# A late output transfer and one more side step between the S5 and dt stages of a hybrid SSD, S5 and attention kernel

## The chip, the cores and the metric

The kernel runs on 1 core of one Trainium2 chip. Its time is the device time of one execution in microseconds (us); the time before is the median of 3 runs.

## What is computed

One layer of a streaming encoder works on 528 prompt rows and 64 sample rows of 1024 channels. After a norm, one wide projection feeds three branches: a Mamba-2 scan (SSD) with heads weighted by `dt`, an S5 state-space branch with a GLU, and stick-breaking attention. The lifted branches are gated and summed, projected back, and followed by an MLP:

```python
y_a, conv_new, ssd_new = ssd_branch(h, ...)
y_b, s5_re, s5_im = s5_branch(h @ col(OFF_U, S5_WIDTH), ...)
glu = jax.nn.gelu(y_b) @ lp['w_glu']
out_b = glu[..., :D_MODEL] * jax.nn.sigmoid(glu[..., D_MODEL:])
o_c = stick_breaking(q, k, v)
mix = (gates[:, :, 0] * (y_a @ lp['w_lift_a']) + gates[:, :, 1] * out_b
       + gates[:, :, 2] * (o_c @ lp['w_lift_c']))
x = x + mix @ lp['w_out']
x = x + jnp.square(jax.nn.relu(rmsnorm(x) @ lp['w_up'])) @ lp['w_down']
```

The states of the branches are outputs too; the final S5 states go out as `s5_out`.

## The kernel before

TensorE works through a list of dense projections (`dense`, L379): each weight tile of 128x1024 is loaded (`w_raw`, L287), split by ScalarE into a high part (`w_hi`, L253) and by VectorE into a low part (`w_lo`, L217), and multiplied in three passes per 128 rows of contraction (L336 to L338), 24 matmuls for a part of 288 columns (12 for the GLU and the attention lift, whose contraction is half as long). Three PSUM buffers (`ps_d`) hold the sums until they are evicted. The order of the projections is: u, q/v/k, then xbc, z and the gates g1, g2, g0, then `glu`, `lc` (the attention lift, input `ocx`), `la` (the SSD lift, inputs `yah` and `yal`), `out`, and the MLP.

The scans and the attention are side work. They are Python generators that yield between steps: `s5_parts`, `s5`, `attention` (which first runs `steps`, the dt sums) and `ssd`. After each dense part, `side` (L373) adds the front generator's pace to a credit and lets it do one step (`pull`) for each whole unit; the paces are 1.25, 1.35, 1.8 and 1.1 (L35). The steps are traced in this order, and a scheduler of the framework then places every instruction into its engine's queue by its own estimate of readiness. What stands in a queue afterwards is therefore not fixed by the source line alone.

The places that the change touches: `s5` computes its end states into `so` (L814 to L816), sends them to `s5_out` (L817), and then runs eight steps `it` that load a tile `tz` from DRAM (L834) and do the last S5 matmuls `ps_y` (L847, L849). `attention` (L885) calls `steps` (L1139): the matmuls of dt (`ps_dt`, L1148), two exponentials on VectorE (`expd`, tiles `ea_` and `ed_`), a softplus (`sp_`), `dta` (L1182) and the dt sums on TensorE (`ps_ac`, L1184 to L1186). Then come four attention tiles, and after them `ssd`: six chunks with `turned`, `decay`, `weigh`, `outputs` (`ps_y`, L1318) and `state`, and between them `gated` and `normed`, which multiply with z, sum squares into `sa`, take a norm by a matmul with ones (`ps_n`, L408) and an rsqrt on ScalarE and VectorE (`rstd_of`, L240 to L247), and scale `ya`. At the end `yah` and `yal` (L257, L258) are split off for `la`:

```python
for g in range(2):
    normed(1, g)
    yield
    for m in range(4 * g, 4 * g + 4):
        scaled_split(ya[:, m, on], sg[:, m:m + 1], yah[:, m, on], yal[:, m, on])
```

The norm matmul occurs four times in `ssd`; the fourth is the last of the side work on TensorE before `la`.

Of the kernel before, what the change touches and what calls it, by code (L numbers as in the profile page):

```python
# [176 lines left out]
def body(tc, io):  # L177
    nc = tc.nc
    V, S, G, PE, SP = nc.vector, nc.scalar, nc.gpsimd, nc.tensor, nc.sync
# [4 lines left out]
    with ExitStack() as ctx:  # L184
# [31 lines left out]
        def tt(e, o, a, b, op):  # L216
            e.tensor_tensor(o, a, b, op=op)  # L217
# [31 lines left out]
        def sigmoid(a, out, scale=1.0):  # L249
            S.activation(out, a, AF.Sigmoid, scale=scale)  # L250
# [469 lines left out]
        def s5():  # L720
# [93 lines left out]
            so = new("so", [128, 4, 16])  # L814
            for j, (xx, c) in enumerate(((x_r, NB), (x_i, NB), (x_r, NX - 1), (x_i, NX - 1))):
                G.tensor_copy(so[:, j, :], xx[:, :, c])  # L816
            SP.dma_start(io["s5_out"], so)  # L817
            yield

            y_sb = sp.tile([128, 32, NY], F32, name="y_sb", tag="yy")  # L820
# [8 lines left out]
            for it in range(8):  # L829
                t0, gl = 4 * (it // 2), it % 2  # L830
                gs = slice(2 * t0 + gl, 2 * t0 + 8, 2)
                tz = sp.tile([128, 4, 128], F32, name="tz", tag="tz%d" % (it % 2))
                for s in range(8):
                    SP.dma_start(tz[16 * s:16 * s + 16, :, :], kv[:, gs, (7 - s) * 16:(7 - s) * 16 + 128])  # L834
                oc = sp.tile([128, 4, 8, 16], F32, name="oc", tag="oc%d" % (it % 2))
                od = sp.tile([128, 4, 8, 16], F32, name="od", tag="od")
                sh = [128, 4, 8, 16]
                for e, o, j in ((V, oc, 0), (G, od, 1)):
                    tt(e, o, p2[j][:, gl, :, t0:t0 + 4].rearrange("p s t -> p t s").unsqueeze(3).to_broadcast(sh),
                       cc[:, j].rearrange("p (h t c) -> p h t c", h=2, c=16)[:, gl, t0:t0 + 4].unsqueeze(2)  # L840
                       .to_broadcast(sh), OP.mult)
                tt(V, oc, oc, od, OP.add)
                yield
                ps = psg.tile([128, 512], F32, name="ps_y5", tag="g")
                for j in range(4):
                    o = ps[:, j * NY:(j + 1) * NY]
                    PE.matmul(o, tz[:, j, :], ub[:, 2 * (t0 + j) + gl, MB + 1:NX], start=True, stop=False,  # L847
                              skip_group_check=True)
                    PE.matmul(o, fs(oc[:, j]), xs[gl][:, t0 + j, MB:NX - 1], start=False, stop=True, skip_group_check=True)  # L849
                yield  # L850
                pv = ps[:, :4 * NY].rearrange("p (g b) -> p g b", b=NY)
                yv = y_sb[:, gs, :]
                c0 = 2.0 * math.sqrt(2.0 / math.pi)
                sq = sp.tile([128, 4 * NY], F32, name="gsq", tag="gsq")
                S.activation(sq, ps[:, :4 * NY], AF.Square)
                V.scalar_tensor_tensor(sq, sq, 1.0 / 0.044715, ps[:, :4 * NY], op0=OP.add, op1=OP.mult)
                sigmoid(sq, sq, 0.044715 * c0)
                tt(V, yv, pv, sq.rearrange("p (g b) -> p g b", b=NY), OP.mult)
                if it % 2:
                    m = it // 2  # L860
                    yo = yb_scr[128 * m:128 * m + 128, :].rearrange("(g c) (s b) -> s c g b", c=16, b=NY)
                    for s in range(8):
                        SP.dma_start(yo[s], y_sb[16 * s:16 * s + 16, 8 * m:8 * m + 8, :])
                yield
# [18 lines left out]


        def attention():  # L885
            yield from steps()
            ap = tc.alloc_tile_pool(name="attn", bufs=2)
            a1 = tc.alloc_tile_pool(name="attn1", bufs=1)
# [534 lines left out]
        n1.release()  # L1423
        do_dt()
        pulls.append((s5(), PACE["s5"]))
        for m in range(4):
            do_qk("q", m, qg, q_scr, live)
            do_v(m)
            do_qk("k", m, kg, io["k_out"], halves)
        pulls.append((attention(), PACE["attention"]))  # L1430
        for n, m in mixed():
            if n == "xbc":
# [229 lines left out]
```

## Time and profile before

| | us |
|---|---|
| median of 3 runs | 1118.86 (1118.25 to 1122.1) |
| profiled execution, device time | 1120.97 |
| its span, first to last instruction | 1119.2 |
| TensorE busy in the span | 1100.5 |
| VectorE busy | 794.3 |
| ScalarE busy | 539.6 |

The span is what the rows below divide up; 1.8 us of the profiled execution lie around it. The profiled execution is 2.1 us above the median of the runs. A busy matmul row lasts about 0.3 us, but they overlap and follow each other at about 0.13 us.

### The profile page before, as it was taken

The numbers are of one execution on the slowest core, as the hardware profiler recorded it, in microseconds if no ns is written. First come the engines' busy times: TensorE is split into PE (matmuls) and PEld (weight loads), VectorE is DVE, ScalarE is ACT, GpSimd is POOL, SyncE is SP. The second block draws the span as 40 slices with busy tenths as digits, with TensorE's granted clock in tenths as the row PEclk, the third lists the DMA queues.
The fourth block names the chain that finished last, engine by engine and source line by source line (L and its number), as shares of the span: only waits on it lengthen the run. The fifth ranks groups of instructions, "written<-read, shape, count | busy, mean of one in ns | idle before, by whom it ended". The sixth has DMA issues, their size and how long they took to land.

```text
span 1119.2 us, 21309 instructions
## 1 busy us (share of the span) xinstructions
PE 1100.5 (98%) x8532; PEld 1061.7 (95%) x8532; DVE 794.3 (71%) x1377; ACT 539.6 (48%) x896; POOL 183.7 (16%) x240
## 2 busy tenths in 40 slices
PE   9999999999999999999998999999999999999998
PEld 8998999999998999898788999999999999999998
DVE  7968579955667475549988754467866785786787
ACT  6455465523365455465668323355444444444443
POOL 2086256611000000005422300300000000000000
PEclk9999999989999999999999999999999999999999
DMA  7663224466754353277445543322232223223222
GB/s 275 147 145 115 84 90 125 110 165 165 241 177 138 113 179 133 89 255 257 129 146 167 151 134 99 99 75 94 76 102 88 75 77 115 74 76 129 79 81 80
DMA packets 80594, 144.04 MB, mean 129 GB/s; under 512 B 26512, under 2 KB 40688, under 8 KB 79984
## 3 DMA queue, kind: packets, MB, share of 16 engines
q1 hardware_dynamic: 80496, 142.69, 41.0%
q8 instruction: 67, 1.10, 0.4%
q14 instruction: 31, 0.25, 0.1%
HBM read 117.40 MB, written 24.38 MB: 127 GB/s over the span
## 4 chain that ended last, share of the span: by engine, by line
PE 80%; DVE 10%; POOL 3%; ACT 2%; DMA 2%; issue 2%; SPq 1%; DVEq 0%; ACTq 0%; POOLq 0%
PE ps_d L336 18%; PE ps_d L337 18%; PE ps_d L338 18%; PE ps_x L1581 3%; PE ps_x L1580 3%; PE ps_x L1582 3%; PE ps_o L895 2%; PE ps_z L895 2%; PE ps_y L1581 1%; PE ps_y L1580 1%; PE ps_y L1582 1%; DVE w_lo L217 1%; DVE ar L1272 1%; DVE ar L217 1%; POOL cm L217 1%
## 5 line engine op out<-in xcount | busy, mean ns | idle before, releaser
L336 PE MATMUL ps_d<-hh,w_hi 128*128 128x288 f32 (+1 forms) x864 | 260.5, 301 | 0.0
L338 PE MATMUL ps_d<-hh,w_lo 128*128 128x288 f32 (+1 forms) x864 | 260.0, 301 | 0.0
L337 PE MATMUL ps_d<-hl,w_hi 128*128 128x288 f32 (+1 forms) x864 | 260.0, 301 | 0.0
L253 ACT ACTIVATE w_hi<-w_raw 128x1024 fp32r<-128x1024 f32 (+1 forms) x150 | 151.8, 1012 | 220.7 <-PE ps_d L337 142.8
L217 DVE TENSOR_TENSOR w_lo<-w_raw,w_hi 128x1024 fp32r<-128x1024 f32 (+1 forms) x150 | 179.2, 1195 | 104.2 <-ACT w_hi L253 103.7
L337 PEld LDWEIGHTS ps_d<-hl,w_hi 128*128 128x128 f32 x864 | 164.5, 190 | 0.9 <-issue 0.3
L338 PEld LDWEIGHTS ps_d<-hh,w_lo 128*128 128x128 f32 x864 | 164.7, 191 | 0.5
L336 PEld LDWEIGHTS ps_d<-hh,w_hi 128*128 128x128 f32 x864 | 164.7, 191 | 0.4
L336 PE MATMUL ps_d<-x2h,w_hi 128*128 128x288 f32 x512 | 151.3, 296 | 0.0
L337 PE MATMUL ps_d<-x2l,w_hi 128*128 128x288 f32 x512 | 151.1, 295 | 0.0
L338 PE MATMUL ps_d<-x2h,w_lo 128*128 128x288 f32 x512 | 150.3, 295 | 0.0
L338 PEld LDWEIGHTS ps_d<-x2h,w_lo 128*128 128x128 f32 x512 | 96.2, 188 | 0.1
L336 PEld LDWEIGHTS ps_d<-x2h,w_hi 128*128 128x128 f32 x512 | 96.2, 188 | 0.1
L337 PEld LDWEIGHTS ps_d<-x2l,w_hi 128*128 128x128 f32 x512 | 96.2, 188 | 0.0
L253 ACT ACTIVATE w_hi<-ws 128x1024 fp32r<-128x1024 f32 x32 | 34.0, 1061 | 55.0 <-PE ps_y L1581 21.7
L1581 PE MATMUL ps_x<-ftl,w_hi 128*128 128x288 f32 x192 | 56.7, 295 | 0.5 <-DVE ftl L217 0.5
L1580 PE MATMUL ps_x<-fth,w_hi 128*128 128x288 f32 x192 | 56.8, 296 | 0.2 <-ACT s L1600 0.2
L1582 PE MATMUL ps_x<-fth,w_lo 128*128 128x288 f32 x192 | 56.4, 294 | 0.0
L1531 ACT ACTIVATE fr<-ps_d 128x288 f32<-128x288 f32 x64 | 25.7, 402 | 55.8 <-PE ps_d L338 55.8
L217 POOL TENSOR_TENSOR xe<-xd,tend 128x1024 f32<-128x1024 f32 (+2 forms) x6 | 11.6, 1942 | 234.4 <-DVE xd L217 210.1
L217 DVE TENSOR_TENSOR w_lo<-ws,w_hi 128x1024 fp32r<-128x1024 f32 x32 | 39.0, 1220 | 12.6 <-ACT w_hi L253 12.6
L906 DVE TENSOR_TENSOR_SCAN aw<-col,aw 128x400 f32<-128x400 f32 (+4 forms) x36 | 30.7, 899 | 17.3 <-ACT aw L250 17.2
(472 smaller groups left out, 2727.1 us busy)
## 6 DMA issues: line engine op xcount, KB each, us to landing
w_raw<-wts SPq DMA_DIRECT2D x150, 512.0 KB, 3.5
g_scr<-go SPq DMA_DIRECT2D x24, 288.0 KB, 2.8
gt<-g_scr SPq DMA_DIRECT2D x24, 288.0 KB, 3.1
ar<-ac_scr SPq DMA_DIRECT2D x4, 1024.0 KB, 7.2
x_scr<-cs SPq DMA_DIRECT2D x10, 297.5 KB, 2.9
xc<-x_scr SPq DMA_DIRECT2D x4, 640.0 KB, 7.0
xt<-xT SPq DMA_DIRECT2D x8, 296.0 KB, 5.7
z_scr<-zs SPq DMA_DIRECT2D x8, 288.0 KB, 4.6
```

Source lines behind the costliest of these rows:

```text
L217: e.tensor_tensor(o, a, b, op=op)
L253: S.activation(hi, x, AF.Copy)
L336: PE.matmul(ps, wh[:, c], xh[:, k, cols], start=start and k == 0, stop=False)
L337: PE.matmul(ps, wh[:, c], xl[:, k, cols], start=False, stop=False)
L338: PE.matmul(ps, wl[:, c], xh[:, k, cols], start=False, stop=stop and k == kt - 1)
L895: mm = lambda *a, **b: PE.matmul(*a, skip_group_check=True, **b)
L906: V.tensor_tensor_scan(x, one.to_broadcast([128, n]), x, 1.0, op0=OP.mult, op1=OP.mult)
L1272: V.tensor_scalar(ar[:n, h, :n], ar[:n, h, :n], acm[:n, c, h:h + 1], 0.0, op0=OP.subtract, op1=OP.min)
L1531: S.activation(r[:, cols], ps, AF.Relu)
L1580: PE.matmul(ps, w[0][:, o], fh[:, k], start=first and k == 0, stop=False, skip_group_check=True)
L1581: PE.matmul(ps, w[0][:, o], fl[:, k], start=False, stop=False, skip_group_check=True)
L1582: PE.matmul(ps, w[1][:, o], fh[:, k], start=False, stop=k == 3, skip_group_check=True)
```

## The change

The call that sends the S5 end states is moved from before the eight S5 steps into the one with `it == 4`, and the attention generator gets one empty step before the dt sums.

```diff
@@ in s5
             for j, (xx, c) in enumerate(((x_r, NB), (x_i, NB), (x_r, NX - 1), (x_i, NX - 1))):
                 G.tensor_copy(so[:, j, :], xx[:, :, c])
-            SP.dma_start(io["s5_out"], so)
             yield
...
                 od = sp.tile([128, 4, 8, 16], F32, name="od", tag="od")
+                if it == 4:
+                    SP.dma_start(io["s5_out"], so)
                 sh = [128, 4, 8, 16]
@@ in attention
         def attention():
+            yield
             yield from steps()
```

In the queues this is what comes of it. On SyncE, where the DMAs are issued, the rows around `s5_out` (its name is `s_out` here, its source `so`), first before:

```order
L287 DMA w_raw<-wts 128x1024
L828 DMA xs_2385<-x_r 64x1216
L828 DMA xs_2384<-x_i 64x1216
L817 DMA s_out<-so 128x64
L287 DMA w_raw<-wts 128x1024
L578 DMA x_scr<-cs 128x595
```

and now, with the line numbers of the changed file:

```order
L287 DMA w_raw<-wts 128x1024
L827 DMA xs_2384<-x_r 64x1216
L827 DMA xs_2383<-x_i 64x1216
L837 DMA s_out<-so 128x64
L287 DMA w_raw<-wts 128x1024
L578 DMA x_scr<-cs 128x595
```

The transfer has kept its place in the queue, the 99th of SyncE's DMAs and branches in both. TensorE's queue also is the same row for row up to and including the dt matmuls `ps_dt`.

On VectorE, between the end of the second exponential (`e_`) and the softplus (`sp_`), before:

```order
L276 SCALAR_TENSOR_TENSOR e_3367<-ed_q,ed_b 128x96
L217 TENSOR_TENSOR w_lo<-w_raw,w_hi 128x1024
L1165 TENSOR_SCALAR s_3368<-e_3367 128x96
L217 TENSOR_TENSOR akcl<-akc,akch 128x512
L1166 RECIPROCAL s_3368<-s_3368 128x96
L217 TENSOR_TENSOR akcl<-aks,akch 128x64
L217 TENSOR_TENSOR qbl<-aqs,qbh 64x64 x2
L217 TENSOR_TENSOR s_3368<-s_3368,e_3367 128x96
L217 TENSOR_TENSOR s_3369<-s_3368 128x96
L1169 TENSOR_SCALAR sp__3394<-s_3369 128x96
L1171 SCALAR_TENSOR_TENSOR sp__3394<-sp__3394,s_3369 128x96 x6
L217 TENSOR_TENSOR w_lo<-w_raw,w_hi 128x1024
```

and now:

```order
L276 SCALAR_TENSOR_TENSOR e_3402<-ed_q,ed_b 128x96
L1167 TENSOR_SCALAR s_3403<-e_3402 128x96
L1168 RECIPROCAL s_3403<-s_3403 128x96
L217 TENSOR_TENSOR s_3403<-s_3403,e_3402 128x96
L217 TENSOR_TENSOR s_3404<-s_3403 128x96
L1171 TENSOR_SCALAR sp__3429<-s_3404 128x96
L1173 SCALAR_TENSOR_TENSOR sp__3429<-sp__3429,s_3404 128x96 x6
L217 TENSOR_TENSOR w_lo<-w_raw,w_hi 128x1024
```

The splits of the first attention tile's sample keys (`akcl`, `qbl`) have left this stretch for a later one, and the chain reaches `dta` one weight split earlier. The two exponentials, which stood one after the other, are now interleaved. On TensorE the dt sums `ps_ac`, and with them the first attention tile, come 48 dense matmuls earlier than before; the four tiles then drift between 60 earlier and 80 later, and the last attention matmul and the first of `ssd` stand 2 earlier than before. From there the SSD outputs `ps_y` stand 17 to 25 dense matmuls later, those of the last chunk 57; the four norm matmuls `ps_n` stand 38, 27, 82 and 55 later, so that 77 dense matmuls lie between the fourth and `la`, where 132 lay before. ScalarE's queue has 37 table loads where it had 35.

On VectorE, at the end of the side work, from the fourth norm (`rsl`) to the last `yal` (`gt<-ps_d` are evictions of `lc`), before:

```order
L246 SCALAR_TENSOR_TENSOR rsl<-ps_n,rsl 128x288
L217 TENSOR_TENSOR gt<-ps_d,gt 128x288
L217 TENSOR_TENSOR w_lo<-w_raw,w_hi 128x1024
L247 SCALAR_TENSOR_TENSOR sa<-rsl,sa 128x288
L217 TENSOR_TENSOR gt<-ps_d,gt 128x288 x2
L217 TENSOR_TENSOR ya<-ya,sa 128x288 x4
L217 TENSOR_TENSOR gt<-ps_d,gt 128x288
L258 SCALAR_TENSOR_TENSOR yal<-ya,sg,yah 128x576 x2
L217 TENSOR_TENSOR gt<-ps_d,gt 128x288
L258 SCALAR_TENSOR_TENSOR yal<-ya,sg,yah 128x576 x2
```

and now:

```order
L246 SCALAR_TENSOR_TENSOR rsl<-ps_n,rsl 128x288
L217 TENSOR_TENSOR w_lo<-w_raw,w_hi 128x1024
L217 TENSOR_TENSOR gt<-ps_d,gt 128x288
L247 SCALAR_TENSOR_TENSOR sa<-rsl,sa 128x288
L217 TENSOR_TENSOR gt<-ps_d,gt 128x288
L217 TENSOR_TENSOR ya<-ya,sa 128x288 x4
L217 TENSOR_TENSOR gt<-ps_d,gt 128x288
L258 SCALAR_TENSOR_TENSOR yal<-ya,sg,yah 128x576
L217 TENSOR_TENSOR gt<-ps_d,gt 128x288
L258 SCALAR_TENSOR_TENSOR yal<-ya,sg,yah 128x576 x2
L217 TENSOR_TENSOR w_lo<-w_raw,w_hi 128x1024
L258 SCALAR_TENSOR_TENSOR yal<-ya,sg,yah 128x576
```

The stretch now starts after the 12th of the 16 `lc` evictions, where it started after the 7th, and the last `yal` stands behind the 16th eviction and one more weight split.

## Rows read from the trace of the kernel before

**Rows 1.** The page, its first part: busy us (share of the span), instructions.

```profile
PE 1100.5 (98%) x8532; PEld 1061.7 (95%) x8532; DVE 794.3 (71%) x1377; ACT 539.6 (48%) x896; POOL 183.7 (16%) x240
```

**Rows 2.** Busy time by stage: stretch, its us, busy us (instructions) by engine, PEclk, DMA.

```profile
core 0: us, PE busy (x) PEld busy (x) DVE busy (x) ACT busy (x) POOL busy (x), PEclk, DMA share, GB/s
225.00:240.00 15.00, 12.58 (x63) 12.38 (x62) 7.69 (x14) 3.60 (x8) 3.81 (x2) 0.66 0.67 179
240.00:310.00 70.00, 69.85 (x531) 69.48 (x530) 40.79 (x110) 20.98 (x43) 6.19 (x8) 0.98 0.67 192
310.00:480.00 170.00, 170.00 (x1437) 157.75 (x1436) 99.75 (x136) 92.37 (x177) 0.00 (x0) 1.00 0.42 135
480.00:640.00 160.00, 152.89 (x1276) 135.23 (x1276) 131.66 (x261) 97.63 (x127) 50.46 (x26) 1.00 0.61 191
```

**Rows 3.** What TensorE waited for: us in total, times, longest.

```profile
PE ps_y L847 <- DMA tz<-kd_scr: 2.4, 1, 2.4
PE ps_d L336 <- DVE mix L217: 2.1, 2, 1.7
...
PE ps_d L336 <- ACT gls L250: 1.3, 2, 1.1
PE ps_d L336 <- ACT sa L244: 1.3, 1, 1.3
PE ps_y L1318 <- DVE ar L217: 1.2, 2, 0.7
PE ps_d L336 <- DVE gt L217: 1.1, 1, 1.1
```

**Rows 4.** VectorE in order of time (start, us), 298 to 309 us, the dt chain.

```profile
298.76 1.23 DVE L217 TENSOR_TENSOR w_lo<-w_raw,w_hi 128x1024 fp32r<-128x1024 f32 x1 [0.98 <-ACT w_hi L253]
...
301.58 0.69 DVE L217 TENSOR_TENSOR akcl<-akc,akch 128x512 fp32r<-128x512 f32 x1 [1.48 <-DMA w_raw<-wts]
...
307.03 0.25 DVE L1171 SCALAR_TENSOR_TENSOR sp__3394<-sp__3394,s 128x96 f32<-128x96 f32 x1
...
308.52 0.26 DVE L217 TENSOR_TENSOR dta<-dt,na 128x96 f32<-128x96 f32 x1
```

**Rows 5.** TensorE in order of time, the dense matmuls 1734 and 1782 of the queue.

```profile
304.73 0.30 PE L336 MATMUL ps_d<-hh,w_hi 128*128 128x288 f32 x1
...
312.32 0.38 PE L336 MATMUL ps_d<-hh,w_hi 128*128 128x288 f32 x1
```

**Rows 6.** Busy time of a stretch between dense work alone, as in Rows 2.

```profile
700.00:728.00 28.00, 28.00 (x213) 28.00 (x212) 13.15 (x19) 9.67 (x13) 9.45 (x5) 1.00 0.32 102
```

**Rows 7.** TensorE, the fourth norm, the start of `la`, and its last `yal` of the first part.

```profile
606.23 0.65 PE L408 MATMUL ps_n<-sa,ones 128*128 128x288 f32 x2
...
627.89 0.33 PE L336 MATMUL ps_d<-yah,w_hi 128*128 128x288 f32 x1
...
630.85 0.29 PE L337 MATMUL ps_d<-yal,w_hi 128*128 128x288 f32 x1
```

**Rows 8.** VectorE, the last of `yal` and a weight split.

```profile
623.07 2.70 DVE L258 SCALAR_TENSOR_TENSOR yal<-ya,sg,yah 128x576 fp32r<-128x576 f32 x2
...
626.06 1.21 DVE L217 TENSOR_TENSOR w_lo<-w_raw,w_hi 128x1024 fp32r<-128x1024 f32 x1
```

**Rows 9.** ScalarE, a table load and a weight split of that stretch.

```profile
609.34 1.28 ACT L243 ACT_TABLE_LOAD   x1
...
622.27 1.04 ACT L253 ACTIVATE w_hi<-w_raw 128x1024 fp32r<-128x1024 f32 x1
```

**Rows 10.** TensorE by 2 us: busy us (matmuls), granted clock, DMA share, GB/s.

```profile
226.00:228.00 2.00, 0.03 (x1) 1.00 0.39 79
...
230.00:232.00 2.00, 2.00 (x11) 0.50 0.95 295
...
592.00:594.00 2.00, 0.46 (x4) 1.00 0.04 12
```

**Rows 11.** TensorE in order of time, the ends of the stretch at the low clock.

```profile
228.86 0.59 PE L338 MATMUL ps_d<-hh,w_lo 128*128 128x288 f32 x1
...
238.47 0.36 PE L338 MATMUL ps_d<-hh,w_lo 128*128 128x288 f32 x1
```

## The prediction

> **What bounds the kernel now.** I read the page's engine line first: TensorE is busy for 1100.5 of the span's 1119.2 us and VectorE for 794.3 [rows 1]. So a change of order can win at most the 18.7 us that TensorE stands idle, and what time it runs at a low clock. Then the busy time by stage, to see where these are [rows 2]. Two places stand out. Around 225 to 240 us TensorE is busy for 12.58 of 15 us and its granted clock is 0.66. In 480 to 640 us, where the SSD side work runs beside the last gates, `glu` and `lc`, TensorE is idle for 7.1 us and VectorE is busy for 131.7 of 160. The attention stage between them has no idle TensorE at all, 170.00 of 170. The list of waits puts names on both [rows 3]: 2.4 us for the S5 tile `tz` in the first place, and in the second `mix` 2.1, `gls` 1.3, `sa` 1.3, `ar` 1.2 and `gt` 1.1, together 7.0 us, all of them results of VectorE or ScalarE. After 640 us the dense work goes on without side work of this kind, and its queues are as they were.
>
> So the kernel runs at TensorE's pace, except in the SSD stretch, where VectorE's queue is nearly full and the two take turns in waiting.
>
> **The moved transfer.** It adds and removes nothing, and in SyncE's queue it stands where it stood, so it passes no other DMA. The `tz` loads and the wait of 2.4 us [rows 3] come ahead of anything that the change reorders, TensorE's queue being the same down to the dt matmuls. Cost 0, with no gain or loss possible from this part.
>
> **The empty step, in the dt chain.** A step that does nothing issues nothing. Its effect is on the order, and the dt sums now stand 48 dense matmuls earlier, at the place of 304.73 us instead of 312.32 [rows 5]. They need `dta`, which was written at 308.52 + 0.26 = 308.78 [rows 4]. Were the chain as long as before, TensorE would wait 308.78 - 304.73 = 4.05 us; that is the upper bound. But the chain has lost what stood in it: the sample keys, whose first split only began at 301.58 after VectorE had waited 1.48 us for a transfer [rows 4], and one weight split. In the new order all of `sp_` but its last seven operations stands ahead of the weight split that ran from 298.76 to 299.99 [rows 4]; what follows that split took, between 307.03 and 308.78 in the old order, 1.8 us (an estimate from the end of the chain in rows 4 and the split ahead of it). So `dta` is ready near 301.8, 2.9 us before it is needed. I take 0. If that cover went, the first attention tile would wait, and since it now starts 6 us earlier than it did, even then nothing behind it would be late.
>
> **The attention tiles.** Their matmuls are dealt out anew among the gate projections, with TensorE never idle in this stage [rows 2]. There is nothing to win, and VectorE (99.8 of 170) and ScalarE (92.4) have room. I take 0.
>
> **The SSD chunks.** From the second chunk on the outputs stand 17 to 25 dense matmuls later. A dense matmul costs 28 us / 213 = 0.13 us [rows 6], so that is 2 to 3 us more for VectorE to get the inputs done, while in VectorE's queue the decay of the next chunk has moved ahead of the weighing of this one: the same work, turned by one step. ScalarE gets two more table loads, at 1.28 us each [rows 9] 2.6 us in a stage where it is busy for 97.6 of 160 us [rows 2]. Bounds: a gain of all 7.0 us of waits [rows 3], a loss of 2.6 us. Since what one wait loses another gains, and VectorE's sum of work is the same, I take 0.
>
> **The end of the side work.** Here the shift is not balanced. Before, the fourth norm ran at 606.23, `la` began at 627.89 and its first part came to the last `yal` at 630.85 [rows 7]; that `yal` was finished at 623.07 + 2.70 = 625.77 [rows 8]. The chain from the norm to the last `yal` thus took 625.77 - 606.23 = 19.5 us and left a margin of 630.85 - 625.77 = 5.1 us. Now 77 dense matmuls lie between the norm and `la` in place of 132: 55 x 0.13 = 7.2 us of cover are gone. If the chain keeps its length, the margin of 5.1 us becomes a wait of 7.2 - 5.1 = **2.1 us** in the first part of `la`. Bounds: below 0, if TensorE arrives at the norm with as much delay as it used to collect behind it; above 2.1 + 1.04 + 1.21 = 4.3 us, if the third weight's split on ScalarE and VectorE [rows 8, 9], which can only run when `lc` has let go of its buffer and now stands ahead of the last `yal`, is added whole to the chain. I take 2.1, the value of the chain as measured, since these splits were in the old chain as well, once.
>
> **The sum.** 0 + 0 + 0 + 0 + 2.1 = +2.1 us on the span of 1119.2. The profiled execution took 1120.97, which is 2.1 us above the median of the runs, 1118.86; against the median the forecast is 1118.86 + 2.1 = **1121.0 us**. About 0.5% (5.6 us) is what a measurement of this kernel can tell from no change; this lies within it.
>
> **Rivals.**
>
> *The clock falls in `la`: slower.* Before, after 2.4 us without a matmul [rows 3, 10], the granted clock went from 1.00 to 0.50, TensorE's lower level of 1.2 GHz, and 11 matmuls instead of some 17 fitted into 2 us; it stayed there from 228.86 to 238.47 [rows 11]. Half of these 9.6 us is lost, 4.8 us. A wait of 1.7 us for `mix` at 592 us [rows 3, 10] left the clock at 1.00. The point from which this decides lies between the two, and my wait of 2.1 us also does, though it may come in pieces between a few matmuls, as the `yal` tiles come one by one. It would then cost 2.1 + 4.8 = 6.9 us: 1125.8. The Trainium skill, "TensorE: Matmul & The Clock Gate", section "HAM oscillation — how this bites in real kernels", tells of the same thing for matmul groups that wait on a DMA: the clock gate falls back to half rate in the gap and the next group starts cold. By that rule a new gap ahead of `la` is paid twice, and the trace agrees at 226 us and not at 592.
>
> *The turn takes the waits out: faster.* Two to three more microseconds before each chunk's outputs would cover each of the single waits for `ar` (longest 0.7), `gls` (1.1) and `mix` (1.7) [rows 3]. If all 7.0 us went and the end of the side work cost nothing, the time would be 1118.86 - 7.0 = 1111.9. Against it speaks that VectorE's share is 82% in this stage [rows 2], so that a wait that is covered at one chunk turns up at the next.
>
> *Nothing that counts: same.* The first half of the change is in fact no change of the queues. If TensorE comes to the fourth norm late enough by itself, the 7.2 us are hidden as well, and the time is 1118.9.
>
> **How the numbers follow.** The chain at the end is measured and the shift is counted, so the forecast has 0.40. Nothing that counts has 0.26, the waits removed 0.18, the clock 0.16. The predicted time is the forecast's, 1121.0. Faster by over 0.5% (below 1113.3) comes from the rival of the removed waits, 0.18; slower (above 1124.5) from the clock rival with 0.16 and 0.01 of the forecast's upper bound, 0.17; the rest is 0.65. The range begins at 1111.9, the time of the removed waits, whose lower half (0.09) is left out, and ends at 1126.5: the clock's 1125.8 is in it, what lies between that and the upper bound of the end together with the clock, 4.3 + 4.8 us or 1128.0, is left out (0.08). Together 0.17 is left out.
>
> **What would show it.** Right: `s5_out` issued at the same place near 230 us and the `tz` wait still 2.4 us; the dt sums without a wait near 305 us; the attention stage still full; TensorE waiting some 2 us for `yal` in the first part of `la`, at about 630 us. Wrong: a stretch at a low clock after 600 us (the clock rival), waits for `mix`, `gls` and `ar` that add up to under 2 us (the fast rival), or a wait at `ps_ac` (the dt chain is longer than I made it). A difference ahead of 280 us would upset the reading of the queues as a whole.

## The result and the profile after

The change makes the kernel slower: 1133.74 us median (1131.82 to 1134.75, 4 runs) against 1118.67 (1118.25 to 1122.1), a ratio of 1.0124 with a 95% interval of 1.0106 to 1.0142, or 15.1 us. The prediction was 1121.0 with a range up to 1126.5. The profiled execution took 1133.86 us with a span of 1132.1, 12.9 more than before; most of the other 2.2 us of the difference of the medians is that the profiled execution of before, 1120.97 us, lay 2.3 us above the median of these runs.

The busy time by stage, in the same stretches as [rows 2]:

```profile
225.00:240.00 15.00, 12.47 (x74) 12.27 (x73) 8.75 (x15) 3.94 (x8) 3.83 (x2) 0.77 0.64 179
240.00:310.00 70.00, 70.00 (x535) 69.74 (x535) 37.43 (x110) 23.26 (x44) 6.18 (x8) 0.98 0.69 192
310.00:480.00 170.00, 170.00 (x1413) 156.08 (x1412) 99.21 (x135) 87.83 (x173) 0.00 (x0) 1.00 0.44 133
480.00:640.00 160.00, 144.96 (x1192) 126.95 (x1191) 130.45 (x246) 96.36 (x125) 43.89 (x25) 0.98 0.56 178
```

In the SSD stretch TensorE is idle for 15.0 us in place of 7.1, and its clock is not full all the time. In the attention stretch it is busy for 170 of 170 us in both kernels, and yet issues 1413 matmuls where it issued 1437; such a window cuts the work at other places than before, so the table below goes by the same matmuls. The waits of TensorE, which answer to [rows 3]:

```profile
PE ps_d L336 <- ACT gls L250: 5.1, 3, 3.0
PE ps_x L1254 <- DVE cb L217: 4.3, 1, 4.3
PE ps_d L336 <- DVE gt L217: 3.9, 3, 2.5
PE ps_y L848 <- DMA tz<-kd_scr: 2.5, 1, 2.5
PE ps_d L336 <- DVE mix L217: 1.6, 1, 1.6
```

The wait for `cb` is new, and so is the long one for `gls`. Where the 12.9 us arose is seen when the start of the same dense matmul (5664 in each trace) is compared with before: its 1700th lies ahead of the dt sums, at its 2600th all attention matmuls are done, from there to the 3200th the SSD chunks run, and by the 3400th the side work is over.

| us added against before | to 1700 | 1700 to 2600, attention | 2600 to 3200, chunks | 3200 to 3400, end |
|---|---|---|---|---|
| the change | -1.8 | +2.9 | +9.1 | +2.8 |

They add up to 13.0. After the 3400th nothing changes. The -1.8 is not the change's: the queues are the same there, and the stretch at the low clock behind the `tz` wait was shorter in this execution, 0.77 in place of 0.66 [rows 2]; the first experiment shows -1.0 with no reordering at all. The three other stages add up to 14.8 us, near the 15.1 us between the medians.

**The chunks.** VectorE, from 503 us on:

```profile
503.36 1.28 DVE L217 TENSOR_TENSOR xd<-ps_x,dt 128x512 f32<-128x512 f32 x2
504.56 10.80 DVE L1274 TENSOR_SCALAR ar<-ar,acm 128x128 f32<-128x128 f32 x16
515.28 0.27 DVE L217 TENSOR_TENSOR cb<-ps_bt,cst 128x128 f32<-128x128 f32 x1
515.48 1.20 DVE L217 TENSOR_TENSOR w_lo<-w_raw,w_hi 128x1024 fp32r<-128x1024 f32 x1
516.62 0.27 DVE L217 TENSOR_TENSOR cb<-ps_bt,cst 128x128 f32<-128x128 f32 x1
```

The 16 small subtractions of `decay` now stand ahead of the second chunk's `cb`, and they take 10.80 us without a pause. Taken one by one, four of them lasted 1.93, 2.43, 1.94 and 2.38 us and the other twelve 0.27 to 0.28. At the same time GpSimd does four operations:

```profile
504.78 2.02 POOL L217 TENSOR_TENSOR xe<-xd,tend 128x1024 f32<-128x1024 f32 x1 [11.59 <-DVE xd L217]
506.75 2.40 POOL L217 TENSOR_TENSOR a<-a,xc 128x1024 f32<-128x1024 f32 x1
509.10 1.91 POOL L217 TENSOR_TENSOR ya<-xc,pa 128x1024 f32<-128x1024 f32 x1
510.96 2.35 POOL L217 TENSOR_TENSOR a<-a,xc 128x1024 f32<-128x1024 f32 x1
```

TensorE has stopped at `ps_x`, whose PSUM buffer is free only when `cb` has been read, and its clock then falls (2 us each: busy us, matmuls, granted clock):

```profile
515.61 0.66 PE L1254 MATMUL ps_x<-cst,xc 128*128 128x128 f32 x4 [4.28 <-DVE cb L217]
```

```profile
512.00:514.00 2.00, 0.00 (x0) 1.00 0.00 0
514.00:516.00 2.00, 0.39 (x4) 1.00 0.00 0
516.00:518.00 2.00, 2.00 (x12) 0.55 0.10 23
518.00:520.00 2.00, 2.00 (x11) 0.60 0.86 294
```

12 and 11 matmuls where 17 fit at 2.4 GHz. One step on, ScalarE meets the exponentials `a` of the third chunk, whose input `ar` is still under way; it waits for the transfer, with an eviction `gls` behind it in its queue for which TensorE stands 3.01 us, and the clock falls once more:

```profile
534.89 1.28 ACT L1272 ACT_TABLE_LOAD   x1 [2.96 <-DMA ar<-ac_scr]
536.19 2.14 ACT L1272 ACTIVATE a<-ar 64x1024 f32<-64x1024 f32 x2
538.34 1.28 ACT L250 ACT_TABLE_LOAD   x1
539.64 0.41 ACT L250 ACTIVATE gls<-ps_d 128x288 f32<-128x288 f32 x1
```

### The profile page after: what moved, and what is told of

Its sections match the earlier page's. It is cut to its first block, busy times and chain, and to the rows that moved or that the text cites. A ratio compares the mean times of both kernels' runs of the same rounds, so it can differ in the third digit from the quotient of the medians.

```text
span 1132.1 us, 21303 instructions
## 1 busy us (share of the span) xinstructions
PE 1104.5 (98%) x8532; PEld 1063.3 (94%) x8532; DVE 802.6 (71%) x1377; ACT 541.8 (48%) x898; POOL 177.9 (16%) x240
## 4 chain that ended last, share of the span: by engine, by line
PE 80%; DVE 10%; POOL 3%; ACT 3%; DMA 2%; issue 2%; SPq 0%; DVEq 0%; ACTq 0%; POOLq 0%
PE ps_d L336 18%; PE ps_d L337 18%; PE ps_d L338 18%; PE ps_x L1583 3%; PE ps_x L1582 3%; PE ps_x L1584 3%; PE ps_o L897 2%; PE ps_z L897 2%; DVE ar L1274 2%; PE ps_y L1583 1%; PE ps_y L1582 1%; PE ps_y L1584 1%; DVE w_lo L217 1%; PE ps_y L1320 1%; POOL cm L217 1%
```

## The experiments

My theory after the result: the empty step turns the SSD steps against the dense work so that a block of 16 small VectorE operations meets four GpSimd operations, each of which holds up one of VectorE's for about its whole length. Rivals: the order alone (the block ahead of `cb`), the attention's new places, the short cover at the end (the prediction's term), a price of the moved transfer. Stage sums below are made as in the table above.

### The transfer alone

```diff
-            SP.dma_start(io["s5_out"], so)
             yield
...
+                if it == 4:
+                    SP.dma_start(io["s5_out"], so)
```

> Only the first half of the change: the s5_out call moved into the step with it == 4, no empty step. Every queue holds the same instructions in the same order as before. Theory of the order (the empty step alone did it): the time of before, 1118.7 us, within 0.2%. Rival (the moved transfer has a price of its own): 1121 us or more, with a longer wait than 2.4 us for tz near 226 us.

Measured: 1120.18 us against 1119.16 for the kernel before beside it, ratio 1.000 (0.9985 to 1.0016). The queues are those of before and so is the time, although the wait for `tz` was 3.3 us in this profile (2.4 in [rows 3], 2.5 in the change). So what the change costs comes from its empty step.

### Four, two and no GpSimd operations beside the block

```diff
-                tt(G, xe[:n], e["xd"][:n], tend[:n, c, :].unsqueeze(2).to_broadcast([n, 16, 64]), OP.mult)
...
+                k = 1 if c == 1 else 64
+                tt(G, xe[:n, :, :k], e["xd"][:n, :, :k], tend[:n, c, :].unsqueeze(2).to_broadcast([n, 16, k]), OP.mult)
```

and `ya` of that chunk in the same manner, in the first of the two kernels also `a` of two chunks. Both kernels thus leave out most of these products; `xe` and `ya` are cleared earlier by two more GpSimd operations.

> The changed kernel with four GpSimd operations cut down: xe and ya of the first 128-row chunk and the products a of the first two compute one column of each head or head dimension (1/64 or 1/128 of the work); xe and ya are cleared earlier, while GpSimd has nothing else to do. So this kernel leaves out most of these four products. The queues of TensorE, VectorE and ScalarE keep their order. Theory of the clash (VectorE's 16 subtractions at 504.6 us took 10.8 us because an operation of GpSimd holds up one of VectorE's while both work on SBUF): the 16 take some 3.3 us, the first cb is there near 508 us, TensorE does not wait 4.3 us at 511 us and its clock does not fall there (4.3 and about 2 us less): 1127.5 us (1125 to 1129.5), with the wait of 3.0 us for gls at 537 us still there, since that is ScalarE waiting for the transfer of ar. Rival 1 (the order alone, the subtractions standing ahead of cb): a block of over 8 us and a wait of over 3 us remain, 1132 to 1135 us. Rival 2 (all later waits only follow from the first): the gls wait goes too, under 1124 us.

> The changed kernel with two of the four GpSimd operations beside the 16 subtractions cut down (xe and ya of the first 128-row chunk, one column of each, so it leaves most of these two products out) and the two products a left whole, 2.4 us each. TensorE's, VectorE's and ScalarE's queues keep their order. Theory of the clash, one VectorE operation held for the whole of each GpSimd operation: the 16 take 3.2 + 2 x 2.2 = 7.6 us (7.0 to 8.0; 10.8 with four, 3.2 with none), the wait for cb at 511 us is 1 to 2 us, too short for the clock to fall: 1127.5 to 1131 us, between the kernel without the four (1127.4) and the changed one (1133.7). Rival (only how much of the time both are at work counts, not the operations): under 6 us for the 16 and no wait, 1126 to 1128 us.

Measured: 1127.4 us (ratio 1.0086, 1.0069 to 1.0103) with none, 1132.14 (1.0108, 1.0081 to 1.0135) with two. The block with none, then with two:

```profile
505.83 3.22 DVE L1278 TENSOR_SCALAR ar<-ar,acm 128x128 f32<-128x128 f32 x16
```

```profile
505.83 7.51 DVE L1278 TENSOR_SCALAR ar<-ar,acm 128x128 f32<-128x128 f32 x16
```

3.22, 7.51 and 10.80 us with no, two and four operations of GpSimd: the two `a`, 2.4 us each, add 2.1 us each, and `xe` and `ya`, 2.0 and 1.9 us, another 1.6 each. That is about the length of each less one small subtraction of 0.2 us. Beside the two `a`, two of the 16 subtractions lasted 2.44 and 2.42 us and the other fourteen 0.27 to 0.29. The order of TensorE, VectorE and ScalarE is the same in all three kernels, so the order alone is ruled out as the cause of the long block, and an even sharing of the time in which both are at work is as well. With none, the wait at `cb` is gone, and the chunks add 1.5 us instead of 9.1: the clash and what follows from it cost 7.6 us. The median fell by only 6.3 us, since the attention stretch of this kernel is 1.2 us longer than that of the change, with a wait of 0.9 us for `aq` that the change does not have. The `gls` wait did not stay at 3.0 as I had written, but shrank to 1.3, so more than half of it was a consequence. With two, `cb` was waited for 1.3 us without a fall of the clock, as expected, but then `gls` for 2.7 us, and the clock fell behind it; the median is 1.1 us above my range.

### The turn of the SSD steps, both ways

```diff
             fetch_chunk(1)
             yield
             yield
-            yield
             turned(0)
```

in the changed kernel, and one `yield` more at this place in the kernel before.

> The changed kernel with one of the three empty steps at the head of ssd taken out, so that the SSD steps come one step sooner again; the dt and attention steps stay shifted as in the change. VectorE's order in the first chunks is then that of before (the first block of 16 subtractions ahead of cb, the second behind the weighing). Theory (the turn of the SSD steps against the dense work is the whole of the loss): no wait over 1.5 us at the second chunk, no wait of 3 us for gls, 1117 to 1122 us. Rival (the dt and attention half of the shift costs): over 1127 us. Rival (only the cover at the end of the side work counts, the prediction's term of 2.1 us): 1131 to 1132 us.

> The kernel before with a fourth empty step at the head of ssd: dt and attention as before, the SSD steps one step later. VectorE then again has 32 subtractions almost in one piece ahead of the second chunk's cb. Theory (the turn of the SSD steps makes the loss): a block of 16 subtractions of 8 us or more under GpSimd's operations and a wait of over 3 us of TensorE at the second chunk, 1127 to 1136 us. Rival (the attention tiles' new places make it): 1117 to 1121 us.

Measured: 1122.64 us (ratio 1.0034, 1.0018 to 1.0049) and 1137.7 (1.018, 1.0164 to 1.0196). With the SSD steps back in their turn, their queue places are those of before, and so are their times: chunks -0.3, end 0.0. What is left is +2.9 in the attention stretch, which is the whole remaining difference in the profile and puts the median 0.6 us over my range. The other kernel has the attention of before (0.0 there) and the block again:

```profile
507.62 10.76 DVE L1272 TENSOR_SCALAR ar<-ar,acm 128x128 f32<-128x128 f32 x16
```

```profile
PE ps_x L1252 <- DVE cb L217: 7.2, 1, 7.2
PE ps_d L336 <- DVE mix L217: 4.3, 1, 4.3
```

TensorE stood for 7.2 us, the clock fell for longer, and the chunks cost 14.9 us, the end 5.2: only 29 dense matmuls lie between the fourth norm and `la` in this kernel, and in `la` TensorE waits 1.5 us for `yah`, as the prediction had it for the change. One step in either kernel decides whether the block meets GpSimd ahead of `cb`. In the order of before the same four GpSimd operations meet a weight split and the two large operations of `weigh` instead; here in the kernel with the SSD steps back in turn:

```profile
506.44 2.10 DVE L217 TENSOR_TENSOR w_lo<-w_raw,w_hi 128x1024 fp32r<-128x1024 f32 x1 [1.02 <-ACT w_hi L253]
...
511.24 5.81 DVE L217 TENSOR_TENSOR ar<-ar,cb 128x1024 f32<-128x1024 f32 x2
516.98 3.21 DVE L1274 TENSOR_SCALAR ar<-ar,acm 128x128 f32<-128x128 f32 x16
```

Undisturbed the split takes 1.22 us and the two products 2.35. Together they lose 0.9 + 3.5 = 4.4 us, of which only the split's 0.9 stand ahead of `cb`; the 16 small ones lose 7.6, all of it ahead of `cb`.

### Two large operations in place of 16 small ones

```diff
-                for h in range(16):
-                    V.tensor_scalar(ar[:n, h, :n], ar[:n, h, :n], acm[:n, c, h:h + 1], 0.0, op0=OP.subtract, op1=OP.min)
+                tt(V, ar[:n, :, :n], ar[:n, :, :n], acm[:n, c, :].unsqueeze(2).to_broadcast([n, 16, n]), OP.subtract)
+                V.tensor_scalar(ar[:n, :, :n], ar[:n, :, :n], 0.0, None, op0=OP.min)
```

> The changed kernel, but the 16 subtractions of a chunk's ar (with the minimum against 0) are two VectorE operations on all 2048 columns, a subtraction and a minimum; the result is the same. TensorE's SSD steps keep their places within 3 dense matmuls. Theory (one VectorE operation at a time waits for one GpSimd operation, so that few large ones are held up less often than 16 small ones): only the subtraction now stands ahead of the second chunk's cb; held up once it ends before TensorE needs cb at 511 us; no wait over 1.5 us there, no fall of the clock: 1124 to 1130 us. Rival (GpSimd's 8.6 us of work are added to VectorE's whatever the size of the operations): the block stays at 10 us and over, the wait at 3 us and over, 1131 us or more.

> The kernel before with the same two large operations in place of 16 small ones. Its subtractions took 22.1 us in the SSD stage, of which about 16.4 by the undisturbed durations (64 x 0.20 and 16 x 0.16 at their pitch, with the ends). Theory: a few us of holding up go, most of it off TensorE's path; the single waits for ar (0.7) and gls may shrink: 1114 to 1119 us. Rival (two passes over 2048 columns cost more than 16 over 128, and wherever GpSimd is at work the long ones are held up as long): 1119 to 1123 us.

Measured: 1134.79 us (1.014, 1.0117 to 1.0164) for the changed kernel with it, 1125.94 (1.0058, 1.0039 to 1.0078) for the kernel before. Both medians lie above the ranges I gave. The first lies in that of its rival, but not for the rival's reason: the subtraction ahead of `cb` takes 2.28 us and nothing waits for `cb`. VectorE and GpSimd then show:

```profile
508.12 2.58 DVE L217 TENSOR_TENSOR w_lo<-w_raw,w_hi 128x1024 fp32r<-128x1024 f32 x1 [0.27 <-ACT w_hi L253]
510.62 0.47 DVE L217 TENSOR_TENSOR cb<-ps_bt,cst 128x128 f32<-128x128 f32 x2
511.02 3.02 DVE L1274 TENSOR_SCALAR ar<-ar 128x2048 f32<-128x2048 f32 x1
```

```profile
505.80 3.82 POOL L217 TENSOR_TENSOR xe<-xd,tend 128x1024 f32<-128x1024 f32 x1 [12.26 <-DVE xd L217]
509.58 3.38 POOL L217 TENSOR_TENSOR a<-a,xc 128x1024 f32<-128x1024 f32 x1
512.92 2.88 POOL L217 TENSOR_TENSOR ya<-xc,pa 128x1024 f32<-128x1024 f32 x1
```

`cb` came in time at 511 us and was not waited for, as the theory had it. But the minimum, 1.2 us by itself, was held to 3.02, ScalarE's exponential of `ar` waited 2.48 us for it, the eviction `go` stood behind that, and TensorE waited 3.8 us for `go`. GpSimd is held too: `xe` took 3.82 us in place of 1.9. Larger operations moved the wait; they did not shorten the whole. In the kernel before, the chunks became 5.7 us slower, with a wait of 3.5 for `st`.

### Two empty steps, and with a longer end

```diff
         def attention():
+            yield
+            yield
             yield from steps()
...
             fetch_chunk(1)
             yield
             yield
-            yield
             turned(0)
```

The second kernel has only the upper half.

> The kernel before with two empty steps ahead of the dt sums (the change has one) and two in place of three at the head of ssd. VectorE's order in the SSD chunks is that of before, without subtractions between the first chunk's and the second's cb; 288 dense matmuls lie between the fourth norm and la (132 before, 77 in the change); the attention's ps_o matmuls come in 20 runs (16 before, 22 in the change). Theory: attention +1.9 us (2.9 us for 6 more runs, in proportion), no clash at the second chunk, the waits at the end of the side work (4.5 us before) shrink by 0 to 4 us: 1116 to 1121 us. Rival (an empty step ahead of dt costs what it cost in the change): 1130 us or more.

> The kernel before with two empty steps ahead of the dt sums and the three at the head of ssd left as they are. VectorE has the 16 subtractions of the second chunk ahead of its cb again, as in the change, but 203 dense matmuls lie between the fourth norm and la (132 before, 77 in the change). Theory (the clash at the second chunk decides, the cover at the end does not): a block of 8 us and over, a wait of TensorE of 3 us and over for the second chunk's cb, 1123 to 1129 us. Rival (the short cover at the end is what made the change slow): 1116 to 1121 us.

Measured: 1127.59 us (1.0075, 1.0048 to 1.0103) and 1134.87 (1.0146, 1.0117 to 1.0175). The two kernels differ in one SSD step, and both have a longer end than before (288 and 203 dense matmuls). The second has the block of 16 ahead of `cb` again, 10.77 us long, and is 7.3 us slower, with these waits:

```profile
PE ps_x L1254 <- DVE cb L217: 3.8, 1, 3.8
...
PE ps_ac L1186 <- DVE dta L217: 2.3, 1, 2.3
```

By stages, the chunks are 5.4 and 7.9 us longer than before and the end is 4.2 us shorter in the first and 0.1 longer in the second, so only 2.5 us of the gap between the two arose in the chunks. What the pair shows is that a short end is not needed for the loss: with a longer end than before, the block and the wait for `cb` are there and the chunks cost 7.9 us. But both are slower than I wrote. With two empty steps the dt sums come before `dta` is ready: 1.8 and 2.3 us, the wait that the prediction bounded and that one step did not bring. And without the block the first kernel loses elsewhere:

```profile
PE ps_d L336 <- ACT gls L250: 8.9, 4, 3.6
```

### GpSimd's product given to ScalarE

```diff
-                tt(G, ya[:, :, t0:t0 + n], e["xc"][:, 0:8, :n], A("d_ssd", 0, 8).unsqueeze(2).to_broadcast([128, 8, n]),
-                   OP.mult)
+                for m in range(8):
+                    S.activation(ya[:, m, t0:t0 + n], e["xc"][:, m, :n], AF.Copy, scale=A("d_ssd", m, 1))
```

in the kernel before.

> The kernel before with the product of xc and d_ssd that starts ya moved from GpSimd (one operation of 1.9 us in each of five chunks) to ScalarE (eight small activations). Attention and the first three chunks keep their places on TensorE. Theory (what GpSimd does beside VectorE in the SSD stage is paid on TensorE's path in the kernel before as well): the weighing of the first chunk falls from 5.8 to under 4.5 us, the waits for ar (1.2 us) and mix (2.1 us) shrink, 1114 to 1118 us, faster than both kernels. Rival (ScalarE's evictions are behind most of what is left, and it gets 2 us more in each chunk): waits for gls and sa grow, 1119 to 1126 us.

Measured: 1131.32 us (1.0104, 1.008 to 1.0127). The weighing fell from 5.81 to 4.13 us, as expected, but the rival's mechanism holds, at more than the price I gave it: the eight activations take 2.44 us of ScalarE's queue per chunk, and TensorE waits 7.9 us for `gls`, once 5.1. No version here beats the kernel before.

## Why the prediction was wrong

*The moved transfer, 0.* Right, shown by the kernel that has it alone.

*The dt chain, 0.* Right, and by its mechanism: `dta` was ready at 299.98 us, 3.0 us before TensorE used it, where the prediction had 2.9.

```profile
299.72 0.26 DVE L217 TENSOR_TENSOR dta<-dt,na 128x96 f32<-128x96 f32 x1
```

```profile
302.98 0.35 PE L1186 MATMUL ps_ac<-dta,cst 128*128 128x96 f32 x2
```

With one more step the wait comes, 1.8 us, within the bound of 4.05.

*The attention tiles, 0: wrong, +2.9.* The step argued that TensorE is never idle there [rows 2]. It is not in the change either; a full share of busy time does not mean that the same matmuls take the same time. The 900 dense matmuls between the 1700th and the 2600th and the 606 of the side work took 179.5 us in the order of before and 182.4 in that of the change, each in four profiles to 0.1 us. What differs is how the `ps_o` matmuls are cut up: before there are 16 runs of them, in the change 22. Within a run they follow each other at 0.065 us on the mean, the first of a run comes 0.22 us after a dense one and the next dense one 0.19 us after the last. By these pitches a further break costs 0.22 + 0.19 - 0.065 - 0.13 = 0.21 us, and six of them 1.3 of the 2.9 us. Summed from one matmul's start to the next, the steps into and out of the runs, 12 more than before, took 2.6 us more, those inside the runs 0.5 more and all others 0.2 less. The kernels with 20 runs lie between: 181 to 182 us, an estimate from their stretch less the SSD matmuls in it, the waits and the time at the low clock. So the loss sits at the runs, but that their number causes it is argued and not shown; no run changed the number alone.

*The SSD chunks, 0 with bounds of -7.0 and +2.6: wrong, +9.1.* This is the step that failed. It said that VectorE's sum of work is the same and that what one wait loses another gains. The sum is not the same: an operation of 0.2 us costs 2 us when GpSimd is at work, and the change moved 16 of them there. The prediction counted VectorE's and ScalarE's queues and left GpSimd's out. GpSimd's own order did not change; the order of the two engines against each other did. The rows that showed the price were in the trace before: beside two GpSimd operations the two products of `weigh` took 5.81 us, where the next chunk's took 2.35:

```profile
508.57 5.81 DVE L217 TENSOR_TENSOR ar<-ar,cb 128x1024 f32<-128x1024 f32 x2
...
525.27 2.35 DVE L217 TENSOR_TENSOR ar<-ar,cb 128x1024 f32<-128x1024 f32 x2
```

```profile
508.08 1.90 POOL L217 TENSOR_TENSOR ya<-xc,pa 128x1024 f32<-128x1024 f32 x1
509.94 3.36 POOL L217 TENSOR_TENSOR a<-a,xc 128x1024 f32<-128x1024 f32 x1
```

7.6 of the 9.1 us are the clash and what follows from it (waits for `cb` and `gls`, two falls of the clock), 1.5 the rest of the turn.

*The end, +2.1: the size nearly right, +2.8, the place not.* `la` started at 640.38 with its inputs ready. The lost cover turned up in the last `lc` parts: an eviction `gt` stands in VectorE's queue behind `rsl`, which waits for ScalarE, and what follows it:

```profile
626.47 0.46 DVE L246 SCALAR_TENSOR_TENSOR rsl<-ps_n,rsl 128x288 f32<-128x288 f32 x1 [1.41 <-ACT rsl L245]
626.97 0.46 DVE L247 SCALAR_TENSOR_TENSOR sa<-rsl,sa 128x288 f32<-128x288 f32 x1
627.43 1.22 DVE L217 TENSOR_TENSOR w_lo<-w_raw,w_hi 128x1024 fp32r<-128x1024 f32 x1
628.57 1.55 DVE L217 TENSOR_TENSOR ya<-ya,sa 128x288 f32<-128x288 f32 x4
630.04 0.81 DVE L217 TENSOR_TENSOR gt<-ps_d,gt 128x288 f32<-128x288 f32 x2
```

TensorE waits 2.52 us for it. With the SSD steps back in turn this stretch costs nothing extra. That the dense matmuls between the fourth norm and `la` are a cover is borne out by the kernels of the experiments: the end costs 5.2 us with 29 of them, 2.7 to 2.9 with 77, nothing with 132, 0.1 with 203, and gains 4.2 with 288. That the wait in `lc` came out near the 2.1 us worked out for `la` is luck: `la` did not wait, and the margin at its last `yal`, from which the 2.1 were worked out, played no part.

*The rivals.* A fall of the clock behind a new wait, the slower rival, did come, but in the chunks, behind waits of 4.3 and 3.0 us, and not in `la`; the 2.52 us ahead of 630.55 left the clock at 1.00, as the 1.7 us for `mix` had [rows 10]. The prediction looked for a length of wait between 1.7 and 2.4 us from which the clock falls. The runs show none: in the second kernel with two empty steps the clock was at its low level soon after waits of 1.6 us (from 542.7) and 1.8 us (from 611.0), in the first it stayed at 1.00 after a wait of 2.7 us for `tz` at 226 us, and in the kernel before it was low from 283.0 to 286.4 us with no wait above 0.15 us in the 25 us ahead, after TensorE had done its last `ps_y` of S5 and `ps_dt`. The waits were not removed. The sign, slower, had a chance of 0.17.

## What to carry to other kernels

When an edit turns two streams of work against each other, list for each engine what the other engines do beside the block that moves, not its own order alone: here a subtraction of 0.27 us took 1.9 us and more beside an operation of GpSimd. And before calling a full stage safe, compare the time between the same two matmuls, not the busy share: 170 of 170 us hid a loss of 2.9.

## What the runs showed of the hardware

In five profiles of whole kernels (before, the change, the transfer alone, and the two with the SSD steps turned), the median subtraction of 128x128 takes 0.27 us alone (294 of them) and 1.93 us beside a GpSimd operation (26, up to 2.48); `st<-st,bd` 0.68 and 1.53, `ar<-ar,cb` 1.21 and 2.48. Operations with one input in PSUM are untouched: `ya<-ps_y,ya` 1.21 and 1.22, `cb<-ps_bt,cst` 0.28 and 0.28. The Trainium skill, "GPSIMD Engine Reference", section "Specifications", says that the two engines share SBUF interfaces, with contention for VectorE instructions in a two-port mode or with two SBUF inputs; "Trainium Architecture — The Big Picture", section "What this means for kernel authors", calls it an exclusive lock and not a split of bandwidth. The trace agrees with both in that the block grew by 1.6 to 2.1 us for each GpSimd operation of 1.9 to 2.4 us, about its whole length, and that operations with an input in PSUM were not held. Which of the two cases the subtraction is, no run here shows.
